# Pool and convolution mixer of a float32 decoder trunk: another order for its second half

## The chip, the cores and the metric

One core of a Trainium2 chip runs the whole program in one launch. The metric is the device time of that launch in microseconds. The engines are TensorE (PE; its weight loads are listed as PEld), VectorE (DVE), ScalarE (ACT), GpSimd (POOL) and SyncE (SP), which here only issues loads. Each engine works through its own list of instructions in order; semaphores tie the lists together.

## The reference, cut to what matters

256 tokens of width 1024 pass two layers in float32: a SwiGLU feed-forward block (FFN), a mixer, another FFN; every part has an RMS norm ahead and adds to the residual `x`. The first layer's mixer is the one that changes:

```python
h = rms_norm(x, mix_norm)
u_pool, u_val, u_gate = split(h @ ab_w_in, (512, 1024))
# pooling: 4 groups of 128 channels, windows 2, 4, 8, 16
mean = trailing_mean(u_pool, window)            # causal
y_pool = einsum('sgc,gcd->sgd', mean - u_pool, pool_w) * pool_scale
# convolution: GLU, depthwise causal conv of 31 taps, LayerNorm over 512 channels, swish
z = conv31(u_val * sigmoid(u_gate), conv_w) + conv_b
mu = mean(z, channels); var = mean((z - mu) ** 2, channels)
y_conv = silu((z - mu) * rsqrt(var + 1e-6) * ln_g + ln_b)
x = x + concat(y_pool, y_conv) @ ab_w_out
```

## The kernel before, in words

**Products in parts.** TensorE multiplies float32 numbers in the faster type fp32r. Each operand is held as a high part (a cast) and a low part (the rest): products high by high, low by high and high by low are summed. So each weight tile takes three steps: the load into `raw` (SyncE), the cast `hi` (ScalarE, L158) and the subtraction `lo` (VectorE, L182). `begin` and `pump` do this. `pump(n)` splits the next n tiles of a fixed list, `stream`, whichever of its two kinds comes next and has a free buffer; `weights(kind)` hands out the next tile and pumps first if it isn't split yet. A tile of kind "gu" (gate/up weights and input projections; 128 x 2048) is split in two halves, one of kind "d" (down and output weights; 128 x 1024) in one piece. There are three raw buffers of each kind, three split ones of "gu" and five of "d". A load is issued when a raw buffer is split (`issue`), a split buffer is free when `done` says that its products are issued and they have run.

**Order.** The schedule is manual: each engine's list has the order in which the code below issues. A `pump` thus puts a cast into ScalarE's list and a subtraction into VectorE's list just where it is called.

**The mixer** (`mixer_ab`, 199 to 289 us). Channels lie on the partitions, tokens along the rows, 128 channels a tile. `wide` makes the first three value/gate pairs; the convolution's taps (L535) run for tile 0, 1, 2, 3 with projections (`narrow_group`, L268) between. `windows` and `pool_diff` (VectorE) make window sums and differences for two pooling groups; `pool_map` (L587, plain float32) maps them, and L591 and L592 scale and split the result into `kh` and `kl`. LayerNorm needs sums over channels, thus over partitions: `mean_mm` (L620) and `variance` (L633) take them on TensorE with a matrix of 1/512, in plain float32. `spread` (L642) brings the reciprocal deviation `r` back to all partitions; `swish` (L656, L658, L652, L653) scales, applies Silu and splits, one token half (`t`) a call. `out_mm(t, k)` adds weight tile k's products (L341) to the accumulators of token half t (two banks each, `a0`, `a1` and `b0`, `b1`): k = 0 to 3 are pooling, 4 to 7 convolution channels, which `tail` does.

**The close and the next FFN.** `tail` finishes token half 0, adds it to `x` (L227, `x_86` and `x_87` are its two column halves), takes sums of squares on ScalarE (L229), `rstd` on GpSimd (L235), `h` on VectorE (L238), and transposes `h` on TensorE (L245) while token half 1's products run; L249 and L252 write the transposed parts into `hT`. Then the next FFN's `wide` starts: first-half-token products of three gate/up tiles (L304), with `finish_b` (the transposes of token half 1) ahead of the third tile, then all of token half 1 (L312) and the low parts (L315).

Of the kernel before, what the change touches and what calls it, by code (L numbers as in the profile page):

```python
# [10 lines left out]
AF = mybir.ActivationFunctionType  # L11
# [28 lines left out]
def tile_trunk(ctx: ExitStack, tc: tile.TileContext, d: dict, out: bass.AP):  # L40
# [20 lines left out]
    def bank(tag):  # L61
        return pspool.tile([P, 512], F32, tag=tag, name=nm(tag), bufs=1)

    def t1():
        return tpool.tile([P, 256], F32, tag="t1", name=nm("t1"), bufs=8)

    def t15():
        return tpool.tile([P, 384], F32, tag="t15", name=nm("t15"), bufs=6)
# [4 lines left out]
    def small(w):  # L73
        return tpool.tile([P, w], F32, tag=f"sm{w}", name=nm("sm"), bufs=8)
# [120 lines left out]
    def done(kind, n=1):  # L195
        spent[kind] += n
# [27 lines left out]
    def norm_half(t, half, accs, coef, ss):  # L224
        x = xs[t][half]
        if accs is not None:
            dve.scalar_tensor_tensor(x, accs[half], coef, x, op0=ALU.mult, op1=ALU.add)  # L227
        junk = tpool.tile([P, 512], F32, tag="bm", name=nm("junk"), bufs=2)
        act.activation(junk, x, AF.Square, scale=1.0 / 32.0, accum_out=ss[:, half:half + 1])  # L229

    def norm_apply(t, ss, g):
        ms = small(1)
        dve.scalar_tensor_tensor(ms, ss[:, 0:1], EPS, ss[:, 1:2], op0=ALU.add, op1=ALU.add)  # L233
        rstd = small(1)
        pool.tensor_tensor(rstd, ms, mhalf[:, 0:1], op=ALU.pow)  # L235
        for half in range(2):
            h = tpool.tile([P, 512], F32, tag="h", name=nm("h"), bufs=4)
            dve.scalar_tensor_tensor(h, xs[t][half], rstd, g[half],  # L238
                                     op0=ALU.mult, op1=ALU.mult)
            yield h  # L240
# [108 lines left out]
    def new_accs():  # L349
        return [[bank(ATAG[t][h]) for h in range(2)] for t in range(2)]  # L350

    def tail(accs, kts, ws, coef, g, units=(1, 1)):

        n = len(kts)

        def mm(t, half, k):
            down_mm(accs[t][half], kts[k], ws[k], t, half, False, k == n - 1)

        ss = small(2)
        for half in range(2):  # L360
            for k in range(n):
                mm(0, half, k)
            pump(units[half])
            norm_half(0, half, accs[0], coef, ss)
        ha = list(norm_apply(0, ss, g))
        for k in range(n):
            mm(1, 0, k)
        for k in range(n):
            mm(1, 1, k)
            if k < 2:  # L370
                transpose_half(0, k, ha, ATAG[0][k])
        done("d", n)
        ss = small(2)
        for half in range(2):
            norm_half(1, half, accs[1], coef, ss)
        hb = list(norm_apply(1, ss, g))

        def finish_b():
            for half in range(2):
                transpose_half(1, half, hb, ATAG[1][half])  # L380
        return finish_b
# [114 lines left out]
    def mixer_ab(finish_b, gname):  # L496
# [13 lines left out]


        where = {}
        ys = [None] * 4
        shifted = {}

# [23 lines left out]
        def taps_out(j):  # L539
            ys[j] = t1()  # L540
            dve.tensor_scalar(ys[j], where[j][:, 0:256], convb[:, j:j + 1], None, op0=ALU.add)

        pw = tpool.tile([P, 512], F32, tag="h", name="pw", bufs=4)
        pool.dma_start(pw, d["pool_w"])
# [66 lines left out]
                done("d")  # L611

        toks = (slice(0, P), slice(P, 2 * P))
        stat = {}

        def mean_mm(js):
            if js[0] == 0:
                stat["mean"] = bank("g2")[:, 0:256]
            for j in js:
                pe.matmul(stat["mean"], ones, ys[j], start=j == 0, stop=j == 3)  # L620

        def squares():
            cs, sqs = [t1() for _ in range(4)], [t15() for _ in range(4)]
            for ts in toks:
                for j in range(4):
                    dve.tensor_tensor(cs[j][:, ts], ys[j][:, ts], stat["mean"][:, ts], op=ALU.subtract)
                    act.activation(sqs[j][:, ts], cs[j][:, ts], AF.Square)
            stat["c"], stat["sq"] = cs, sqs

        def variance(t, tag):  # L630
            var = bank(tag)
            for j in range(4):
                pe.matmul(var[:, 0:1], stat["sq"][j][:, toks[t]], ones[:, 0:1], start=j == 0, stop=j == 3)  # L633
            ve = small(1)
            dve.tensor_scalar(ve, var[:, 0:1], EPS, None, op0=ALU.add)
            r = small(1)
            pool.tensor_tensor(r, ve, mhalf[:, 0:1], op=ALU.pow)
            stat["r", t] = r

        def spread(t, tag):  # L640
            rb = bank(tag)
            pe.matmul(rb[:, 0:P], stat["r", t].to_broadcast([P, P]), ident, start=True, stop=True)  # L642
            stat["rb", t] = rb

        def swish(t):
            ts = toks[t]
            cs, rb = stat["c"], stat["rb", t]
            ss = []

            def lows(j):  # L650
                hi, lo = kts[4 + j]
                (act.copy if j % 2 else dve.tensor_copy)(hi[:, ts], ss[j])  # L652
                dve.tensor_tensor(lo[:, ts], ss[j], f32(hi[:, ts]), op=ALU.subtract)  # L653

            for j in range(4):
                dve.tensor_tensor(cs[j][:, ts], cs[j][:, ts], rb[:, 0:P], op=ALU.mult)  # L656
                s = t1()[:, 0:P]
                act.activation(s, cs[j][:, ts], AF.Silu, scale=lng[:, j:j + 1], bias=lnb[:, j:j + 1])  # L658
                ss.append(s)
                if t == 0:  # L660
                    kts.append(new_split())
                if j >= LAG:
                    lows(j - LAG)
            for j in range(4 - LAG, 4):
                lows(j)
# [27 lines left out]
        taps_pe(1, "b1")  # L693
        taps_out(1)
        load_pack(3)
        p23 = project("a1")
        windows(2, p23)
        taps_pe(2, "b0")
        taps_out(2)
        pump(1)  # L700
        g = load_gain(gname)
        pool_diff(2)
        taps_pe(3, "g1")
        mean_mm((0, 1, 2))
        pump(1)
        taps_out(3)
        preload(AF.Silu)
        p01 = project("g0")
        mean_mm((3,))
        pool_map(2, "g3")  # L710
        squares()
        windows(0, p01)
        variance(0, "g1")
        out_mm(0, 0)
        out_mm(1, 0)
        variance(1, "g2")
        pool_diff(0)
        out_mm(0, 1)
        out_mm(1, 1)
        pool_map(0, "g0")  # L720
        spread(0, "g3")
        spread(1, "g1")
        pump(1)
        swish(0)
        out_mm(0, 2)
        out_mm(1, 2)
        pump(1)
        out_mm(0, 3)
        out_mm(1, 3)
        swish(1)  # L730
        pump(2)
        accs = [accs[0], accs[1]]
        return tail(accs, kts[4:8], [weights("d") for _ in range(4)], 1.0, g, (0, 0))


    def bias_rows(tag):
# [414 lines left out]
```

## Time and profile before

| what | value |
|---|---|
| runs | 990.82, 995.86, 996.42 us (median 995.86) |
| profiled execution, its own time | 993.01 us |
| its span | 991.2 us |
| TensorE, VectorE, ScalarE busy | 98%, 66%, 54% of the span |
| mixer's second half, from the last taps to FFN 1's first matmul | 243.8 to 289.2 us |

[...] Idle time in brackets is the time in which the engine stood still, with the engine and line that ended it.

### The profile page before, as it was taken

The page shows a single profiled execution, that of the slowest core. Times are in us where ns is not written, and L with a number is a line of the kernel's source. Part 1 is how long each engine was busy: PE and PEld are TensorE (multiplying, and loading weights), DVE is VectorE, ACT ScalarE, POOL GpSimd, SP SyncE. Part 2 cuts the span into 40 slices and gives each one's busy share as a digit, 9 for nine tenths or more (in the row PEclk, how much of TensorE's full clock was granted, in tenths as well). Part 3 has the DMA queues.
Part 4 walks back from the last instruction along what each step waited for, and adds up shares of the span by engine and source line. Part 5 has one row for each costly group of instructions (what it writes and reads, how often), then busy time and mean ns, then how long its engine had stood idle before and what let it go on. Part 6 is the DMA issues. An engine that isn't in the chain of part 4 may idle for free.

```text
span 991.2 us, 14724 instructions
## 1 busy us (share of the span) xinstructions
PE 968.1 (98%) x5738; PEld 839.5 (85%) x5738; DVE 657.3 (66%) x1086; ACT 534.0 (54%) x959; POOL 62.9 (6%) x90
## 2 busy tenths in 40 slices
PE   7999999999889999999999999999999999999997
PEld 6888888897769888888988888888889798888885
DVE  6876666678367766666686666667888668666653
ACT  5665555465356655555565555545456646555542
POOL 3000000000000010000000000000435000000000
PEclk9999999999999999999999999999999999999999
DMA  9875555435136656655365555437444616655401
GB/s 332 311 270 191 191 191 191 171 119 173 61 110 240 244 213 237 237 192 206 121 247 209 191 191 191 161 107 264 146 138 157 211 66 242 240 184 195 159 1 43
DMA packets 38021, 182.03 MB, mean 184 GB/s; under 512 B 6416, under 2 KB 6448, under 8 KB 24768
## 3 DMA queue, kind: packets, MB, share of 16 engines
q1 hardware_dynamic: 32400, 169.92, 48.0%
q0 software_dynamic: 5264, 10.92, 3.4%
q8 instruction: 45, 0.74, 0.3%
q10 hardware_dynamic: 288, 0.27, 0.1%
q14 instruction: 24, 0.20, 0.1%
HBM read 179.92 MB, written 4.22 MB: 186 GB/s over the span
## 4 chain that ended last, share of the span: by engine, by line
PE 92%; DVE 3%; issue 2%; ACT 1%; DMA 1%; POOL 0%; SPq 0%; POOLq 0%; DVEq 0%; ACTq 0%
PE g L284 29%; PE g L287 15%; PE a L341 14%; PE b L341 13%; PE g L268 4%; PE g L312 2%; PE g L315 2%; PE g L304 2%; PE a L268 1%; PE b L535 1%; DVE lo L182 1%; PE a L315 1%; PE a L312 1%; PE b L811 1%; DVE keep L957 1%
## 5 line engine op out<-in xcount | busy, mean ns | idle before, releaser
L182 DVE TENSOR_TENSOR lo<-raw,hi 128x1024 fp32r<-128x1024 f32 (+1 forms) x319 | 380.4, 1243 | 56.3 <-ACT hi L158 56.3
L158 ACT CAST hi<-raw 128x1024 fp32r<-128x1024 f32 x320 | 314.8, 1043 | 5.3 <-DMA raw<-in_c_out 3.4
L284 PE MATMUL g<-hT,hi 128*128 128x512 f32 x1248 | 310.7, 391 | 0.8 <-DVE t L327 0.8
L284 PEld LDWEIGHTS g<-hT,hi 128*128 128x128 f32 x1248 | 228.7, 188 | 44.8 <-DVE t L327 1.0
L324 ACT COPY t<-g 128x256 f32<-128x256 f32 x174 | 63.4, 372 | 221.1 <-PE g L287 205.6
L287 PEld LDWEIGHTS g<-hT,lo 128*128 128x128 f32 x1248 | 170.3, 190 | 12.2
L287 PE MATMUL g<-hT,lo 128*128 128x256 f32 x1248 | 174.0, 282 | 0.0
L327 DVE TENSOR_TENSOR t<-g,t 128x256 f32<-128x256 f32 x174 | 71.7, 420 | 137.3 <-ACT t L324 137.3
L341 PE MATMUL a<-hi,kh 128*128 128x512 f32 x208 | 83.4, 401 | 2.8 <-ACT hi L158 2.7
L341 PE MATMUL a<-lo,kh 128*128 128x512 f32 x208 | 82.8, 398 | 1.2 <-DVE lo L182 1.2
L341 PE MATMUL b<-hi,kh 128*128 128x512 f32 x208 | 82.3, 396 | 0.0
L341 PE MATMUL a<-hi,kl 128*128 128x512 f32 x208 | 81.8, 393 | 0.0
L341 PE MATMUL b<-hi,kl 128*128 128x512 f32 x208 | 81.5, 392 | 0.0
L341 PE MATMUL b<-lo,kh 128*128 128x512 f32 x208 | 81.5, 392 | 0.0
L390 ACT CAST kh<-t 128x256 fp32r<-128x256 f32 x88 | 35.7, 406 | 57.6 <-DVE t L388 57.6
L391 DVE TENSOR_TENSOR kl<-t,kh 128x256 fp32r<-128x256 f32 x88 | 37.4, 425 | 41.5 <-ACT kh L390 41.5
L386 ACT ACTIVATE t<-t 128x256 f32<-128x256 f32 x88 | 36.9, 420 | 26.7 <-DVE t L327 26.6
L235 POOL TENSOR_TENSOR sm<-sm,mhalf 128x1 f32<-128x1 f32 x11 | 6.1, 556 | 673.3 <-DVE sm L233 673.3
L341 PEld LDWEIGHTS a<-hi,kh 128*128 128x128 f32 x208 | 39.6, 191 | 10.0 <-ACT hi L158 3.1
L341 PEld LDWEIGHTS a<-hi,kl 128*128 128x128 f32 x208 | 39.5, 190 | 9.0 <-DVE kl L592 0.2
L341 PEld LDWEIGHTS b<-hi,kl 128*128 128x128 f32 x208 | 39.3, 189 | 8.3
L341 PEld LDWEIGHTS b<-hi,kh 128*128 128x128 f32 x208 | 39.4, 189 | 8.2
(208 smaller groups left out, 953.4 us busy)
## 6 DMA issues: line engine op xcount, KB each, us to landing
raw<-in_gu SPq DMA_DIRECT2D x87, 1024.0 KB, 4.9
raw<-in_dn SPq DMA_DIRECT2D x88, 512.0 KB, 5.4
raw<-in_c_qk SPq DMA_DIRECT2D x8, 1024.0 KB, 4.9
raw<-in_ab_in SPq DMA_DIRECT2D x6, 1024.0 KB, 4.8
raw<-in_ab_out SPq DMA_DIRECT2D x8, 512.0 KB, 5.6
raw<-in_c_v SPq DMA_DIRECT2D x8, 512.0 KB, 4.3
raw<-in_c_out SPq DMA_DIRECT2D x8, 512.0 KB, 4.2
eall<-escr POOLq DMA_DIRECT2D x4, 768.0 KB, 17.1
```

The costliest lines, as they stand in the source:

```text
L158: act.copy(hi[:, c], raws[k][:, c])
L182: e.tensor_tensor(lo[:, c], raws[k][:, c], f32(hi[:, c]), op=ALU.subtract)
L268: pe.matmul(dst, wt[:, c, cols], hT[:, c, part, :], start=n == 0, stop=n == len(seq) - 1)
L284: pe.matmul(b, hi[:, c, cols], hT[:, c, 0:2, :], start=c == 0, stop=False, skip_group_check=True)
L287: pe.matmul(b[:, 0:256], lo[:, c, cols], hT[:, c, 0, :], start=False, stop=c == NCH - 1, skip_group_check=True)
L312: pe.matmul(bv[:, :, P:2 * P], w[0][:, c, cs], hT[:, c, 0:2, P:2 * P], start=False, stop=False, skip_group_check=True)
L324: act.copy(t[:m], bv[:, 1, :])
L327: dve.tensor_tensor(dst[:m], bv[:, 0, :], t[:m], op=ALU.add)
L341: pe.matmul(acc, kt[a][:, ts], w[b][:, hs], start=start and n == 0, stop=stop and n == 2)
L386: act.activation(s, gv, AF.Silu)
L390: act.copy(hi, m)
L391: dve.tensor_tensor(lo, m, f32(hi), op=ALU.subtract)
```

## The change

Five things change, all in `mixer_ab` and in the `tail` that it calls. The channel sum of the four convolution tiles is made by adds on VectorE in `taps_out`, and `mean_mm` is one product of that sum; `squares` and `variance` do the same for the squares, on all 256 tokens at once, with the centred values written over `ys`. The last projection's two halves have the first `pool_map` and the mean between them. The second `pool_map` stands between the two token halves of `out_mm(·, 1)`. All four casts in `swish` are ScalarE's, and `swish(1)` stands ahead of `out_mm(·, 3)` in the code. Splits move: one "d" tile ahead of the window sums, none behind `swish(1)`, and `tail` has a new argument, `between`, that pumps one tile behind the first half of the residual sum (other calls of `tail` leave it at 0).

```diff
-    def tail(accs, kts, ws, coef, g, units=(1, 1)):
+    def tail(accs, kts, ws, coef, g, units=(1, 1), between=0):
...
             norm_half(0, half, accs[0], coef, ss)
+            if half == 0:
+                pump(between)
...
         def taps_out(j):
             ys[j] = t1()
             dve.tensor_scalar(ys[j], where[j][:, 0:256], convb[:, j:j + 1], None, op0=ALU.add)
+            if j == 1:
+                stat["sum"] = t1()
+            if j:
+                dve.tensor_tensor(stat["sum"], stat["sum"] if j > 1 else ys[0], ys[j], op=ALU.add)
...
-        def mean_mm(js):
-            if js[0] == 0:
-                stat["mean"] = bank("g2")[:, 0:256]
-            for j in js:
-                pe.matmul(stat["mean"], ones, ys[j], start=j == 0, stop=j == 3)
+        def mean_mm(tag):
+            stat["mean"] = bank(tag)[:, 0:256]
+            pe.matmul(stat["mean"], ones, stat["sum"], start=True, stop=True)
         def squares():
-            cs, sqs = [t1() for _ in range(4)], [t15() for _ in range(4)]
-            for ts in toks:
-                for j in range(4):
-                    dve.tensor_tensor(cs[j][:, ts], ys[j][:, ts], stat["mean"][:, ts], op=ALU.subtract)
-                    act.activation(sqs[j][:, ts], cs[j][:, ts], AF.Square)
-            stat["c"], stat["sq"] = cs, sqs
+            cs, sqs = ys, []
+            for j in range(4):
+                dve.tensor_tensor(cs[j], ys[j], stat["mean"], op=ALU.subtract)
+                sq = t15()[:, 0:256]
+                act.activation(sq, cs[j], AF.Square)
+                sqs.append(sq)
+                if j % 2:
+                    dve.tensor_tensor(sqs[j - 1], sqs[j - 1], sqs[j], op=ALU.add)
+            dve.tensor_tensor(sqs[0], sqs[0], sqs[2], op=ALU.add)
+            stat["c"], stat["sq"] = cs, sqs[0]
-        def variance(t, tag):
+        def variance(tag):
             var = bank(tag)
-            for j in range(4):
-                pe.matmul(var[:, 0:1], stat["sq"][j][:, toks[t]], ones[:, 0:1], start=j == 0, stop=j == 3)
-            ve = small(1)
-            dve.tensor_scalar(ve, var[:, 0:1], EPS, None, op0=ALU.add)
-            r = small(1)
-            pool.tensor_tensor(r, ve, mhalf[:, 0:1], op=ALU.pow)
-            stat["r", t] = r
+            for t in range(2):
+                pe.matmul(var[:, t:t + 1], stat["sq"][:, toks[t]], ones[:, 0:1], start=True, stop=True)
+            ve = small(2)
+            dve.tensor_scalar(ve, var[:, 0:2], EPS, None, op0=ALU.add)
+            r = small(2)
+            pool.tensor_tensor(r, ve, mhalf, op=ALU.pow)
+            stat["r"] = r
...
-                (act.copy if j % 2 else dve.tensor_copy)(hi[:, ts], ss[j])
+                act.copy(hi[:, ts], ss[j])
...
         load_pack(3)
+        pump(1)
         p23 = project("a1")
         windows(2, p23)
         taps_pe(2, "b0")
+        pool_diff(2)
         taps_out(2)
-        pump(1)
         g = load_gain(gname)
-        pool_diff(2)
         taps_pe(3, "g1")
-        mean_mm((0, 1, 2))
-        pump(1)
         taps_out(3)
         preload(AF.Silu)
-        p01 = project("g0")
-        mean_mm((3,))
+        last = weights("gu")
+        b01 = bank("g0")
+        p01 = b01[:, 0:256], b01[:, 256:512]
+        narrow_group(p01[0], last, slice(0, P))
         pool_map(2, "g3")
+        mean_mm("g2")
+        narrow_group(p01[1], last, slice(P, 2 * P))
+        done("gu")
         squares()
-        windows(0, p01)
-        variance(0, "g1")
         out_mm(0, 0)
         out_mm(1, 0)
-        variance(1, "g2")
+        windows(0, p01)
+        variance("g2")
+        out_mm(0, 1)
         pool_diff(0)
-        out_mm(0, 1)
+        pump(1)
+        pool_map(0, "g3")
         out_mm(1, 1)
-        pool_map(0, "g0")
-        spread(0, "g3")
-        spread(1, "g1")
+        spread("g1")
+        swish(0)
         pump(1)
-        swish(0)
         out_mm(0, 2)
         out_mm(1, 2)
         pump(1)
+        swish(1)
         out_mm(0, 3)
         out_mm(1, 3)
-        swish(1)
-        pump(2)
         accs = [accs[0], accs[1]]
-        return tail(accs, kts[4:8], [weights("d") for _ in range(4)], 1.0, g, (0, 0))
+        return tail(accs, kts[4:8], [weights("d") for _ in range(4)], 1.0, g, (0, 0), 1)
```

The lists of three places follow. TensorE behind the last taps, up to the first output products (`g` and `a` are banks, `t` tiles of 256 columns, `kh` and `kl` the split input of a product), before:

```order
L620 MATMUL g_449_2540<-t_419_2274,ones 128x256
L620 MATMUL g_449_2540<-t_426_2381,ones 128x256
L620 MATMUL g_449_2540<-t_439_2487,ones 128x256
L268 MATMUL g_455_2556<-hT,hi_2233 128x256 x16
L268 MATMUL g_455_2556<-hT,lo_2236 128x256 x8
L268 MATMUL g_455_2556<-hT,hi_2233 128x256 x16
L268 MATMUL g_455_2556<-hT,lo_2236 128x256 x8
L620 MATMUL g_449_2540<-t_453_2552,ones 128x256
L587 MATMUL g_456_2606<-t_444_2497,pw 128x256
L587 MATMUL g_456_2606<-t_446_2502,pw 128x256
L633 MATMUL g_474_2653<-ones,t_465_2621 128x1
```

and with the change:

```order
L268 MATMUL g_452_2548<-hT,hi_2233 128x256 x16
L268 MATMUL g_452_2548<-hT,lo_2236 128x256 x8
L594 MATMUL g_453_2573<-t_443_2495,pw 128x256
L594 MATMUL g_453_2573<-t_445_2500,pw 128x256
L624 MATMUL g_458_2584<-t_427_2383,ones 128x256
L268 MATMUL g_452_2548<-hT,hi_2233 128x256 x16
L268 MATMUL g_452_2548<-hT,lo_2236 128x256 x8
L341 MATMUL a_463_2625<-hi_1855,kh_2576 128x512
```

The first map and the one mean product now have half of the projection behind them, and the variance stands behind twelve output products.

VectorE at the mixer's close, from the last low part of `swish(1)` to the norm's `h`, before (`lo_2810` is the last output weight, `lo_2817` a gate/up tile of FFN 1):

```order
L653 TENSOR_TENSOR kl_2751<-t_516_2800,kh_2750 128x128
L182 TENSOR_TENSOR lo_2810<-raw_2493,hi_2808 128x1024
L182 TENSOR_TENSOR lo_2817<-raw_2173,hi_2814 128x1024 x2
L227 SCALAR_TENSOR_TENSOR x_86<-a_477_2662,x_86 128x512
L227 SCALAR_TENSOR_TENSOR x_87<-a_478_2663,x_87 128x512
L233 SCALAR_TENSOR_TENSOR sm_2853<-sm_2822 128x1
L238 SCALAR_TENSOR_TENSOR h_2857<-x_86,sm_2855,gain_2495 128x512
```

and with the change (`lo_2805` is the first gate/up tile of FFN 1):

```order
L664 TENSOR_TENSOR kl_2723<-t_509_2766,kh_2722 128x128
L227 SCALAR_TENSOR_TENSOR x_86<-a_463_2625,x_86 128x512
L182 TENSOR_TENSOR lo_2805<-raw_2106,hi_2802 128x1024 x2
L227 SCALAR_TENSOR_TENSOR x_87<-a_464_2626,x_87 128x512
L233 SCALAR_TENSOR_TENSOR sm_2825<-sm_2786 128x1
L238 SCALAR_TENSOR_TENSOR h_2829<-x_86,sm_2827,gain_2508 128x512
```

The splits ahead of `x_86` are gone, and one stands between `x_86` and `x_87`.

VectorE between the norm of token half 1 and its transposed low part, before:

```order
L238 SCALAR_TENSOR_TENSOR h_2910<-x_88,sm_2908,gain_2495 128x512
L238 SCALAR_TENSOR_TENSOR h_2912<-x_89,sm_2908,gain_2495 128x512
L182 TENSOR_TENSOR lo_2917<-raw_2239,hi_2914 128x1024 x2
L252 TENSOR_TENSOR hT<-b_546_2958,hT 128x4x128
L252 TENSOR_TENSOR hT<-b_547_2965,hT 128x4x128
```

and with the change:

```order
L238 SCALAR_TENSOR_TENSOR h_2882<-x_88,sm_2880,gain_2508 128x512
L238 SCALAR_TENSOR_TENSOR h_2884<-x_89,sm_2880,gain_2508 128x512
L182 TENSOR_TENSOR lo_2889<-raw_2173,hi_2886 128x1024 x2
L182 TENSOR_TENSOR lo_2897<-raw_2239,hi_2894 128x1024 x2
L252 TENSOR_TENSOR hT<-b_539_2938,hT 128x4x128
L252 TENSOR_TENSOR hT<-b_540_2945,hT 128x4x128
```

Two gate/up tiles are split there, where one was; ScalarE's list has their casts in the same place.

## Rows read from the trace of the kernel before

**Rows 1.** The page: span, TensorE's busy time and instructions, gate/up loads (issue to landing, us).

```profile
span 991.2 us, 14724 instructions
...
PE 968.1 (98%) x5738; PEld 839.5 (85%) x5738; DVE 657.3 (66%) x1086; ACT 534.0 (54%) x959; POOL 62.9 (6%) x90
...
raw<-in_gu SPq DMA_DIRECT2D x87, 1024.0 KB, 4.9
```

**Rows 2.** TensorE's timeline behind the last taps: start, duration, instruction, [idle before, releaser].

```profile
243.81 1.56 PE L620 MATMUL g<-t,ones 128*128 128x256 f32 x6
245.03 2.27 PE L268 MATMUL g<-hT,hi 128*128 128x256 f32 x16
...
251.40 1.02 PE L587 MATMUL g<-t,pw 128*128 128x256 f32 x4
255.07 1.05 PE L633 MATMUL g<-ones,t 128*128 128x1 f32 x8 [2.65 <-ACT t L627]
```

**Rows 3.** TensorE's timeline at the mixer's close and FFN 1's start.

```profile
273.53 0.50 PE L341 MATMUL a<-lo,kh 128*128 128x512 f32 x1 [0.47 <-DVE lo L182]
...
276.96 0.50 PE L341 MATMUL a<-hi,kh 128*128 128x512 f32 x1 [2.70 <-ACT hi L158]
278.22 0.80 PE L341 MATMUL a<-lo,kh 128*128 128x512 f32 x1 [0.76 <-DVE lo L182]
...
280.09 0.63 PE L341 MATMUL a<-hi,kl 128*128 128x512 f32 x1
280.52 0.63 PE L341 MATMUL a<-hi,kh 128*128 128x512 f32 x1
...
282.18 0.39 PE L341 MATMUL a<-hi,kh 128*128 128x512 f32 x1
282.40 0.39 PE L341 MATMUL a<-lo,kh 128*128 128x512 f32 x1
...
286.26 0.63 PE L245 MATMUL a<-ident,h 128*128 128x128 f32 x4
...
289.24 4.00 PE L304 MATMUL g<-hT,hi 128*128 128x256 f32 x32
...
296.59 1.34 PE L312 MATMUL g<-hT,hi 128*128 128x256 f32 x8 [0.32 <-DVE hT L252]
```

**Rows 4.** Stretches: length, busy (count) PE PEld DVE ACT POOL, granted clock, DMA, GB/s.

```profile
257.00:259.00 2.00, 2.00 (x7) 1.55 (x6) 0.00 (x0) 0.00 (x0) 0.00 (x0) 0.55 0.03 8
...
279.00:281.00 2.00, 2.00 (x7) 1.54 (x6) 2.00 (x3) 0.00 (x0) 0.00 (x0) 0.50 0.86 246
```

**Rows 5.** VectorE's timeline in the same part of the mixer.

```profile
246.47 0.48 DVE L541 TENSOR_SCALAR t<-g,cpk 128x256 f32<-128x256 f32 x1
...
254.00 0.48 DVE L592 SCALAR_TENSOR_TENSOR kl<-g,cpk,kh 128x256 fp32r<-128x256 f32 x1 [0.54 <-ACT kh L591]
...
268.76 0.67 DVE L656 TENSOR_TENSOR t<-t,g 128x128 f32<-128x128 f32 x3
...
269.86 0.29 DVE L653 TENSOR_TENSOR kl<-t,kh 128x128 fp32r<-128x128 f32 x1
...
276.94 3.50 DVE L182 TENSOR_TENSOR lo<-raw,hi 128x1024 fp32r<-128x1024 f32 x3 [0.19 <-ACT hi L158]
...
283.06 0.69 DVE L227 SCALAR_TENSOR_TENSOR x<-a,x 128x512 f32<-128x512 f32 x1 [2.02 <-PE a L341]
...
295.85 1.28 DVE L252 TENSOR_TENSOR hT<-b,hT 128x512 fp32r<-128x512 f32 x2
```

**Rows 6.** ScalarE's timeline there.

```profile
269.07 1.81 ACT L658 ACTIVATE t<-t,cpk 128x128 f32<-128x128 f32 x4 [1.49 <-DVE t L656]
270.79 0.48 ACT L652 CAST kh<-t 128x128 fp32r<-128x128 f32 x2
...
283.78 0.63 ACT L229 ACTIVATE junk<-x 128x512 f32<-128x512 f32 x1 [1.99 <-DVE x L227]
...
291.30 1.99 ACT L158 CAST hi<-raw 128x1024 fp32r<-128x1024 f32 x2
```

More of the change, by code (lines that the diff above doesn't have):

```diff
@@ L512, in mixer_ab @@
         where = {}
+        stat = {}
         ys = [None] * 4
@@ L613, in mixer_ab @@
         toks = (slice(0, P), slice(P, 2 * P))
-        stat = {}
-        def mean_mm(js):
-            if js[0] == 0:
-                stat["mean"] = bank("g2")[:, 0:256]
-            for j in js:
-                pe.matmul(stat["mean"], ones, ys[j], start=j == 0, stop=j == 3)
-        def squares():
-            cs, sqs = [t1() for _ in range(4)], [t15() for _ in range(4)]
-            for ts in toks:
-                for j in range(4):
-                    dve.tensor_tensor(cs[j][:, ts], ys[j][:, ts], stat["mean"][:, ts], op=ALU.subtract)
-                    act.activation(sqs[j][:, ts], cs[j][:, ts], AF.Square)
-            stat["c"], stat["sq"] = cs, sqs
@@ L630, in variance @@
-        def variance(t, tag):
-            var = bank(tag)
-            for j in range(4):
-                pe.matmul(var[:, 0:1], stat["sq"][j][:, toks[t]], ones[:, 0:1], start=j == 0, stop=j == 3)
-            ve = small(1)
-            dve.tensor_scalar(ve, var[:, 0:1], EPS, None, op0=ALU.add)
-            r = small(1)
-            pool.tensor_tensor(r, ve, mhalf[:, 0:1], op=ALU.pow)
-            stat["r", t] = r
-        def spread(t, tag):
+        def mean_mm(tag):
+            stat["mean"] = bank(tag)[:, 0:256]
+            pe.matmul(stat["mean"], ones, stat["sum"], start=True, stop=True)
@@ L641, in spread @@
+        def variance(tag):
+            var = bank(tag)
+            for t in range(2):
[5 more added lines that the diff above has]
+            stat["r"] = r
+        def spread(tag):
             rb = bank(tag)
-            pe.matmul(rb[:, 0:P], stat["r", t].to_broadcast([P, P]), ident, start=True, stop=True)
@@ L643, in spread @@
-            stat["rb", t] = rb
+            for t in range(2):
+                pe.matmul(rb[:, toks[t]], stat["r"][:, t:t + 1].to_broadcast([P, P]), ident,
+                          start=True, stop=True)
+            stat["rb"] = rb
         def swish(t):
             ts = toks[t]
-            cs, rb = stat["c"], stat["rb", t]
+            cs, rb = stat["c"], stat["rb"]
             ss = []
@@ L651, in lows @@
                 hi, lo = kts[4 + j]
-                (act.copy if j % 2 else dve.tensor_copy)(hi[:, ts], ss[j])
+                act.copy(hi[:, ts], ss[j])
                 dve.tensor_tensor(lo[:, ts], ss[j], f32(hi[:, ts]), op=ALU.subtract)
             for j in range(4):
-                dve.tensor_tensor(cs[j][:, ts], cs[j][:, ts], rb[:, 0:P], op=ALU.mult)
+                dve.tensor_tensor(cs[j][:, ts], cs[j][:, ts], rb[:, ts], op=ALU.mult)
                 s = t1()[:, 0:P]
```

## Prediction

> **What bounds the kernel now.** I read the page first, for who is busy: TensorE works 968.1 of 991.2 us [rows 1], so nearly everywhere a change counts only if it takes work or a wait off TensorE. Next comes TensorE's timeline over the stretch that the diff touches, from the last taps (243.8) to the first matmuls of FFN 1 (L304 at 289.24) [rows 2, 3]. The brackets there are what to look at. TensorE stands still four times: 2.65 us ahead of the variance column (for the squares), then 0.47, 2.70 and 0.76 us ahead of the last output products (for the splits of the last two output weights): 6.6 us. [...] Last come VectorE's and ScalarE's timelines over the same stretch [rows 5, 6], because whoever releases those waits is the bound as soon as TensorE is no longer it.
>
> Behind 296.59 TensorE runs on without gaps, so I take the whole effect to be the shift of that matmul (L312), the first that needs the second token half of FFN 1's input.
>
> **The change on TensorE.** Removed: the four waits, 6.6. The low clock: about 13 products at 0.43 in place of 0.22, so 2.6 to 2.8. Six of the eight passes of the channel mean: the six in front took 243.81 to 245.03, so 1.2. Twelve of the sixteen passes of the variance: eight take 1.05 [rows 2], so 1.5. In all 11.9. The two spreads stay four passes, the two maps stay eight, the output products stay 96. Splitting the projection around map and mean, and the output product around the second map, changes between operand kinds a few times more; the dearest such change seen is about 0.2 (the first sixteen projection matmuls take 2.27 behind the mean, against 4.00 for 32 in L304), so 0 to 0.4, and I take nothing. Were TensorE alone the bound, L304 would start at 277.3.
>
> **What VectorE and ScalarE make of it.** TensorE's own times in the new order, from rows of before: at 243.8 the projection's halves with two mean passes between (251.40 less 245.03, 6.4), the first map 0.9, twelve output products 2.8, four variance passes 0.5, six products 1.5, which is 255.9; then the second map 0.95, six products 1.5 and the spread 0.6 [rows 2, 3]. First half: VectorE gets three adds of about 0.4 and the split of one output weight (1.2) ahead of the last `taps_out`, and loses the two halves of a gate/up split (2.4) there; it ended this at 246.95 [rows 5] and so ends about as early, while TensorE asks for the channel sum only after one projection half and the first map, at about 247.6. Hidden. The first map's scaling takes 2.06 from its end to the last low part (252.42 to 254.48 [rows 2, 5]) and in the new order lies beside the second projection half. The squares follow: four subtractions, four squares, three adds, about 3.7 to 253.4, beside the first twelve output products, which end at about 254.0. So the 2.65 wait goes, with 0.6 to spare. The second map needs the differences at about 256.1 and TensorE comes there at 255.9: 0.1 to 0.2 wait, 0 to 1 by the error of this walk.
>
> From there I follow the path that ends last. Second map's end 257.05, its scaling 2.06, TensorE's spread at 259.1: the first `swish` starts at 259.1. Inside it all four casts are now ScalarE's. From the rows of one `swish` before [rows 5, 6]: the first Silu starts 0.31 after the first product, Silus follow 0.39 apart, the first cast ends at 1.8, its low part (0.29) at 2.1; only then does VectorE reach the fourth product, which stands behind that low part; its Silu ends at 2.85, three casts 0.2 apart at 3.4, the last low part at 3.7. Casts and low parts of the last two output weights come next, 1.0 and 1.2 apart: the second `swish` starts 6.7 after the first, and VectorE reaches the residual sum of token half 0 (`x_86`) at 259.1 + 6.7 + 3.7 = 269.5, though TensorE, with 36 products of 0.228 behind the spread, had that accumulator ready at 267.5. This is the new bound.
>
> Next the split that `between` adds. `x_86` 0.69, its sum of squares 0.72, the two casts 2.0, the second low half 1.2, and small hand-overs: `x_87`, queued behind `lo_2805` on VectorE, starts 4.8 after `x_86`, at 274.3, where TensorE's accumulator has been ready since 270.1. What is queued behind it are the norm, `h`, and TensorE's transposes. In the trace of before, from `x_87` to the transposes is 283.06 to 286.26, 3.2 [rows 3, 5]: they start at 277.4 or 277.5. TensorE is there at 273.5: **a new wait of 3.9**. From the transposes to L304 is 2.98 before, so L304 starts at 280.4: 8.8 earlier than 289.24, not 11.9.
>
> Last the wide stage of FFN 1. One gate/up tile was cast far ahead and one at the mixer's end; now two of three are split between the second norm and its transposes. ScalarE starts these casts 2.06 after L304 (291.30 less 289.24 [rows 3, 6]): the second tile's halves are there at 3.1 and 4.05, the third's at 5.95. TensorE ends the first tile at 1.9, so it waits 1.2 and 0.5. On VectorE two pairs of low halves (2.3 each) stand ahead of the transposed half's low part where one stood; one pair ended at 295.85, 6.6 after L304, so two end at 8.95, and L312, 0.7 to 0.75 behind that, stands 9.65 after L304, against 7.35 before [rows 3, 5]. **2.3 given back.**
>
> Clock: the 3.9 wait is longer than the two that each had a low stretch behind them, so I expect one here. It would lie over the last products and the first tile of L304; the tile's 1.9 lost falls into the 1.7 that TensorE waits anyway, and up to 0.9 of the transposes' side does not. I take 0.3 (0 to 1).
>
> [...]
>
> DMA: the fourth gate/up tile is now asked for only when `lo_2805` frees its buffer, near 273.5, where it was asked for some 27 earlier, and the next two near 287 and 289. They are cast from about 296 on; the profile page's landing time for these loads is 4.9 [rows 1], so they hide. The down-projection loads start earlier than before, since the output weights are split earlier.
>
> Sum: 8.8 - 2.3 - 0.3 = 6.2 earlier. The profiled execution took 993.0 (its span and 1.8 around it), so its like would take 986.8. The three runs have their median 2.9 above it, at 995.86; against that median 6.2 gives **989.7**.
>
> **Rivals.** One: TensorE stays the bound to the end (11.9, so 984.0). It needs `x_86` at the accumulator's end and the added split hidden. For it: VectorE and ScalarE have idle time in these windows. Against: `x_87` is behind `lo_2805` in VectorE's own order, which no idle time elsewhere mends. Two: the first half doesn't come free. If the squares or the second map's differences come 2 later than walked (their prices here are from like forms, no row has them), the variance and the map wait, and everything on the path moves: 4 left, 992. Three, slower than before: the low clock stays. Three waits in 15 us (3.9, 1.7, 1.1) keep TensorE from a closed run of work, and from 277 to 308, where before it ran through the wide stage at full clock, it runs at half: 144 matmuls of 0.12 more each are 17.3, less the 2.8 of waits that this swallows, so 14.5 given back against 6.2 gained: 1004. It decides from the point where the low stretch lasts over some 19 us. Against: both low stretches of before ended after 3 to 4 us, with the engine working as it will here. [...]
>
> **How the numbers follow.** The forecast 0.66 (gain of 4 to 9, for walk errors of a microsecond or two and a low stretch that costs 0 to 1.4); rival one 0.15; rival two 0.14 (gain of 1 to 4); rival three 0.05. The range runs from rival one's 984.0 to rival two's far part, 993.5. About 1% (10 us) is what a measurement of this kernel tells from no change. Over 1% faster: rival one, the forecast's upper edge and the runs' own spread (990.8 to 996.4), 0.24. Over 1% slower: rival three, 0.05. Within: 0.71.
>
> **What would show it.** Right: no wait at the variance, none at the last output products, a quarter of the passes of mean and variance; one wait of 3 to 4 ahead of the first transposes, released by VectorE's `h`; waits for ScalarE's `hi` inside L304 and for VectorE's `hT` at L312, 1 to 1.5 each. Wrong in the path: `x_87` starting within a microsecond of its accumulator, or L304 before 278.5. Wrong in the first half: a wait of more than 1 at variance, second map or spread. Wrong in the cover: a DMA as releaser at a gate/up cast of FFN 1. Wrong in the clock: a granted clock under 0.7 that lasts past L312.

## The result, and the profile after

| | before | changed |
|---|---|---|
| median of 8 runs each | 994.79 us (990.82 to 996.42) | 988.47 us (986.96 to 989.70) |
| profiled execution, its own time | 993.01 | 987.02 |
| its span | 991.2 | 985.3 |

The ratio is 0.994, 95% interval 0.9925 to 0.9955: 6.3 us faster by the medians. The forecast was 989.7 (6.2 faster) in a range of 984.0 to 993.5. The two profiled executions differ by 6.0.

TensorE's timeline of the changed kernel from the last taps to L312, in the columns of [rows 2, 3]:

```profile
243.87 2.18 PE L268 MATMUL g<-hT,hi 128*128 128x256 f32 x16
...
247.72 0.59 PE L624 MATMUL g<-t,ones 128*128 128x256 f32 x2
...
253.77 0.50 PE L642 MATMUL g<-ones,t 128*128 128x1 f32 x4
...
258.23 0.61 PE L652 MATMUL g<-ident,sm 128*128 128x128 f32 x4
...
277.18 0.66 PE L245 MATMUL a<-ident,h 128*128 128x128 f32 x4 [4.03 <-DVE h L238]
...
281.78 2.06 PE L304 MATMUL g<-hT,hi 128*128 128x256 f32 x16
284.48 0.74 PE L304 MATMUL g<-hT,hi 128*128 128x256 f32 x4 [0.64 <-ACT hi L158]
285.43 1.70 PE L304 MATMUL g<-hT,hi 128*128 128x256 f32 x12 [0.21 <-ACT hi L158]
...
291.02 1.33 PE L312 MATMUL g<-hT,hi 128*128 128x256 f32 x8 [1.11 <-DVE hT L252]
```

None of the four waits of before is left (their brackets at 255.07, 273.53, 276.96 and 278.22 in [rows 2, 3]). In their place stand one of 4.03 at the transposes and three small ones in FFN 1's wide stage. The spread starts at 258.23, L304 at 281.78 in place of 289.24 and L312 at 291.02 in place of 296.59.

VectorE's timeline there, to lay beside [rows 5]:

```profile
258.99 0.67 DVE L667 TENSOR_TENSOR t<-t,g 128x128 f32<-128x128 f32 x3
...
269.32 0.69 DVE L227 SCALAR_TENSOR_TENSOR x<-a,x 128x512 f32<-128x512 f32 x1
271.74 2.36 DVE L182 TENSOR_TENSOR lo<-raw,hi 128x1024 fp32r<-128x1024 f32 x2 [1.73 <-ACT hi L158]
274.01 0.68 DVE L227 SCALAR_TENSOR_TENSOR x<-a,x 128x512 f32<-128x512 f32 x1
```

The first `swish` starts at 258.99, `x_86` at 269.32; then VectorE stands still for 1.73 us until the cast of the added split is there, splits for 2.3, and only then takes `x_87`. The chain that ended last (start, length, what) goes the same way: from the first swish to the transposes it runs through VectorE, ScalarE and GpSimd, without TensorE. Its part around the added split:

```profile
269.32 0.70 DVE x L227
...
270.04 0.72 ACT junk L229 x2
270.76 0.95 ACT hi L158
...
271.74 2.36 DVE lo L182 x2
274.10 0.61 DVE x L227
```

The stretches behind the 4.03 wait, in the columns of [rows 4], show the low clock again, 0.50 from 279 to 281:

```profile
277.00:279.00 2.00, 1.82 (x9) 1.49 (x10) 1.30 (x3) 0.59 (x1) 0.00 (x0) 0.74 0.63 258
279.00:281.00 2.00, 2.00 (x8) 1.71 (x7) 0.76 (x2) 0.59 (x1) 0.00 (x0) 0.50 0.00 0
281.00:283.00 2.00, 2.00 (x15) 1.81 (x14) 1.40 (x3) 0.96 (x3) 0.00 (x0) 0.91 0.00 0
```

### The profile page after: what moved, and what is told of

Same layout as the page of the kernel before. It is cut to its first block, busy times and chain, and to the rows that moved or that the text cites. A ratio compares the mean times of both kernels' runs of the same rounds, so it can differ in the third digit from the quotient of the medians.

```text
span 985.3 us, 14682 instructions
## 1 busy us (share of the span) xinstructions
PE 963.4 (98%) x5720; PEld 836.3 (85%) x5720; DVE 658.6 (67%) x1083; ACT 534.3 (54%) x959; POOL 62.3 (6%) x89
## 4 chain that ended last, share of the span: by engine, by line
PE 92%; DVE 4%; ACT 2%; issue 2%; DMA 0%; POOL 0%; SPq 0%; POOLq 0%; DVEq 0%; ACTq 0%
PE g L284 29%; PE g L287 15%; PE a L341 14%; PE b L341 13%; PE g L268 4%; PE g L312 2%; PE g L315 2%; PE g L304 2%; PE a L268 1%; DVE lo L182 1%; PE b L538 1%; PE a L312 1%; PE a L315 1%; PE b L823 1%; DVE keep L969 1%
## 5 line engine op out<-in xcount | busy, mean ns | idle before, releaser
L341 PEld LDWEIGHTS b<-hi,kh 128*128 128x128 f32 x208 | 39.4, 189 | 8.2
L341 PEld LDWEIGHTS b<-lo,kh 128*128 128x128 f32 x208 | 39.4, 189 | 7.8
```

The costliest lines, as they stand in the source:

```text
L341: pe.matmul(acc, kt[a][:, ts], w[b][:, hs], start=start and n == 0, stop=stop and n == 2)
```

## The experiments

Executions differ by up to 2 us in how late the kernel gets going (the last taps end between 243.8 and 245.8), and by as much behind L312 (692.6 to 694.6 us from there to the end of the span), without relation to the edits. So the times of the stretch are given from the end of the last taps, P (the start of TensorE's next product), in one profiled execution each, and go by starts: output products listed at 0.39 start 0.22 apart (282.18 and 282.40 in [rows 3]); the medians and ratios to the kernel before, each with runs of it on the same chip, stand beside them.

The part behind L312 can be read from the traces. At 705 to 725 us, in the second layer's mixer, TensorE waits about 0.9 and then 1.1 us in all twelve traces (in casts_alt the second in two pieces). In six (before, changed, no_between, sums_on_pe, after_old_splits, early_late) a stretch at the low clock follows, and 694.0 to 694.6 us lie between L312 and the end; in the other six none follows, and it is 692.6 to 693.1. The changed kernel and filler in the same 2 us (length, busy (count) of PE, PEld, DVE, ACT and POOL, granted clock, DMA, GB/s):

```profile
715.00:717.00 2.00, 2.00 (x10) 1.94 (x10) 2.00 (x2) 1.29 (x4) 1.15 (x1) 0.50 0.29 100
```

```profile
715.00:717.00 2.00, 2.00 (x18) 2.00 (x18) 2.00 (x1) 1.07 (x4) 1.02 (x1) 1.00 0.24 86
```

The spread of the runs behind the medians goes with the clock as well: over the 30 executions of the kernel before that were measured beside the experiments, spans of 989.5 to 994.7 us go with a mean granted clock of 0.993 to 0.988, and their product stays within 981.6 to 983.6.

| kernel | P | P to L304 | P to L312 | median, us | ratio, 95% interval |
|---|---|---|---|---|---|
| before | 243.81 | 45.43 | 52.78 | 994.8 to 995.5 | |
| changed | 243.87 | 37.91 | 47.15 | 988.47 | 0.994 (0.9925 to 0.9955) |
| early_split | 245.20 | 32.25 | 41.93 | 981.68 | 0.9866 (0.9851 to 0.9882) |
| no_between | 244.66 | 35.37 | 44.18 | 984.68 | 0.9894 (0.9879 to 0.9910) |
| sums_on_pe | 245.78 | 41.62 | 50.91 | 991.21 | 0.9961 (0.9946 to 0.9975) |
| casts_alt | 244.64 | 35.06 | 44.74 | 984.22, one run | |
| before_splits | 245.09 | 46.25 | 55.59 | 995.63 | 1.0008 (0.9995 to 1.0021) |
| after_old_splits | 245.10 | 39.45 | 46.85 | 986.81 | 0.9924 (0.9901 to 0.9947) |
| filler | 244.89 | 36.33 | 46.00 | 985.36 | 0.9901 (0.9882 to 0.9920) |
| early_late | 244.10 | 32.25 | 40.65 | 981.59 | 0.9870 (0.9848 to 0.9892) |
| early_late_alt | 243.94 | 32.11 | 40.52 | 980.38 | 0.9856 (0.9834 to 0.9878) |
| cast_ahead | 244.12 | 32.13 | 39.07 | 977.84 | 0.9830 (0.9811 to 0.9848) |

**early_split: who makes the new wait.** Against the changed kernel:

```diff
         taps_out(3)
+        pump(1)
         preload(AF.Silu)
...
-        return tail(accs, kts[4:8], [weights("d") for _ in range(4)], 1.0, g, (0, 0), 1)
+        return tail(accs, kts[4:8], [weights("d") for _ in range(4)], 1.0, g, (0, 0), 0)
```

> The split of FFN 1's first gate/up tile moves from between x_86 and x_87 to the 2.3 us in which VectorE waits for the first map (246.1 to 248.4 in the changed kernel's trace); nothing else changes. My theory (the changed kernel's 4.03 us wait ahead of the transposes is that split standing in front of x_87): x_87 starts behind its accumulator at about 270.3 in place of 274.0, the wait ahead of the transposes is under 0.5, the low clock behind it is gone, L304 starts at about 276.7 in place of 281.8, L312 9.7 later, and the time is 4 to 5 us under the changed kernel's 988.5. Rival (x_86 is late because of the second swish, and that makes the wait): the wait stays at 2 or more and the gain is under 2 us.

VectorE's `x_86` and `x_87` are now one piece, and TensorE's transposes have no bracket (one row of VectorE's timeline, then TensorE's):

```profile
270.65 1.28 DVE L227 SCALAR_TENSOR_TENSOR x<-a,x 128x512 f32<-128x512 f32 x2
```

```profile
274.43 0.66 PE L245 MATMUL a<-ident,h 128*128 128x128 f32 x4
...
277.45 2.08 PE L304 MATMUL g<-hT,hi 128*128 128x256 f32 x16
280.58 0.74 PE L304 MATMUL g<-hT,hi 128*128 128x256 f32 x4 [1.05 <-ACT hi L158]
...
287.13 1.34 PE L312 MATMUL g<-hT,hi 128*128 128x256 f32 x8 [1.10 <-DVE hT L252]
```

The 4.03 wait is gone whole, L312 comes 5.2 earlier than in the changed kernel. The median is 6.8 lower, where 4 to 5 was expected; the 1.6 over the stretch's 5.2 lie outside it. `x_86` starts as late after P as there (25.45 in both), so the second swish is not what makes the wait: the rival falls. L312 stands 9.68 behind L304, as the prediction's 9.65 had it for a full clock; the granted clock is 1.00 here from 274 to 285.

**no_between: the same split left to FFN 1's start.**

```diff
-        return tail(accs, kts[4:8], [weights("d") for _ in range(4)], 1.0, g, (0, 0), 1)
+        return tail(accs, kts[4:8], [weights("d") for _ in range(4)], 1.0, g, (0, 0), 0)
```

> The split between x_86 and x_87 is left out there and so falls to FFN 1's start, where three gate/up tiles are then split in a row. My theory: the wait ahead of the transposes goes as well (under 0.5), but TensorE now waits some 3 us at L304 for the first cast, and three pairs of low halves stand ahead of the transposed half's low part, so that L312 starts 12 us behind L304 in place of 9.3: L312 at about 289 in place of 291, 1 to 2 us faster than the changed kernel. Rival (the second swish makes the wait, and the split is free cover there): the wait stays, and the third split at FFN 1's start makes it 2 to 3 us slower than the changed kernel.

TensorE's timeline has its one long wait at L304 now, for the first cast:

```profile
280.03 0.74 PE L304 MATMUL g<-hT,hi 128*128 128x256 f32 x4 [2.97 <-ACT hi L158]
280.98 5.11 PE L304 MATMUL g<-hT,hi 128*128 128x256 f32 x28 [0.21 <-ACT hi L158]
288.84 1.34 PE L312 MATMUL g<-hT,hi 128*128 128x256 f32 x8
```

L312 3.0 earlier than in the changed kernel where 1 to 2 was expected: three late splits instead of two still cost less than the one between `x_86` and `x_87`. L312 is 8.8 behind L304, since TensorE's wait now lies ahead of L304, and has no wait of its own.

**sums_on_pe: the channel sums back on TensorE.**

```diff
-            pe.matmul(stat["mean"], ones, stat["sum"], start=True, stop=True)
+            for j in range(4):
+                pe.matmul(stat["mean"], ones, ys[j], start=j == 0, stop=j == 3)
...
-                pe.matmul(var[:, t:t + 1], stat["sq"][:, toks[t]], ones[:, 0:1], start=True, stop=True)
+                for j in range(4):
+                    pe.matmul(var[:, t:t + 1], stat["sq"][j][:, toks[t]], ones[:, 0:1],
+                              start=j == 0, stop=j == 3)
```

(and the six adds in `taps_out` and `squares` left out.)

> The channel sums of values and squares go back to TensorE (four products each that add up in the bank), with every other part of the change kept. My theory: TensorE's work from the last taps to the first swish grows by six mean passes (1.2) and twelve variance passes (1.4), all of it on the path that ends last, so the first swish and all behind it come 2.5 later and the time is 2 to 3 us over the changed kernel's. Rival (VectorE is the bound over this whole stretch, and six adds of 0.4 leave it): no slower, or up to 2 us faster than the changed kernel.

TensorE's timeline:

```profile
249.63 1.89 PE L621 MATMUL g<-t,ones 128*128 128x256 f32 x8
...
256.98 1.84 PE L637 MATMUL g<-ones,t 128*128 128x1 f32 x16
...
281.80 1.11 PE L245 MATMUL a<-ident,h 128*128 128x128 f32 x4 [4.05 <-DVE h L238]
...
287.40 2.18 PE L304 MATMUL g<-hT,hi 128*128 128x256 f32 x16
```

Eight and sixteen passes in place of two and four; a float32 product of 256 columns (two passes) takes 0.39 here, four in 249.63 to 251.17, and one in fp32r 0.13, sixteen of L268 in 251.17 to 253.27. `x_86` comes 28.15 after P (273.93) in place of 25.45: 2.7 later, as expected, and the median is 2.7 over the changed kernel's. In the trace L312 is 3.8 later; the 1.0 more lies between transposes and L304, 5.6 in place of 4.6: the granted clock is at 0.50 from 281 to 287, about twice as long as in the changed kernel.

**casts_alt: the swishes' length.**

```diff
-                act.copy(hi[:, ts], ss[j])
+                (act.copy if j % 2 else dve.tensor_copy)(hi[:, ts], ss[j])
```

> In swish the casts alternate between VectorE and ScalarE again, as in the kernel before; all else as in the changed kernel. My theory (the two swishes lie on the path that ends last, and ScalarE's casts make each 0.4 longer): x_86 starts 0.6 to 0.9 earlier than 269.3, and L304 and L312 by about as much. Rival (they do not lie on it): L304 and L312 stay within 0.2 of 281.8 and 291.

VectorE's and TensorE's row:

```profile
268.83 0.69 DVE L227 SCALAR_TENSOR_TENSOR x<-a,x 128x512 f32<-128x512 f32 x1
```

```profile
276.69 0.66 PE L245 MATMUL a<-ident,h 128*128 128x128 f32 x4 [2.73 <-DVE h L238]
...
279.70 2.07 PE L304 MATMUL g<-hT,hi 128*128 128x256 f32 x16
```

`x_86` 24.19 after P in place of 25.45: 1.3 earlier, more than the 0.6 to 0.9 expected: ScalarE also reaches the next weight casts sooner, 2.1 behind the first swish's first Silu (262.18 less 260.07) in place of 3.0 (262.31 less 259.31). The wait falls from 4.03 to 2.73 and no low stretch follows it (1.00 granted from 274 to 285): from the transposes to L304 3.0 in place of 4.6. So L312 gains 2.4, of which 1.3 is the swishes and the rest the clock. Its time is that of a single run, so the reading rests on the trace.

**before_splits and after_old_splits: one half of the change without the other.** The first is the kernel before with the new places of the splits alone; the second is the changed kernel with the places as before. The edit of the first (with `between` added to `tail` as in the change; the second takes the same lines back):

```diff
         load_pack(3)
+        pump(1)
...
         taps_out(2)
-        pump(1)
...
         mean_mm((0, 1, 2))
-        pump(1)
...
         out_mm(0, 1)
+        pump(1)
         out_mm(1, 1)
...
-        pump(1)
         swish(0)
+        pump(1)
         out_mm(0, 2)
         out_mm(1, 2)
         pump(1)
+        swish(1)
         out_mm(0, 3)
         out_mm(1, 3)
-        swish(1)
-        pump(2)
...
-        return tail(accs, kts[4:8], [weights("d") for _ in range(4)], 1.0, g, (0, 0))
+        return tail(accs, kts[4:8], [weights("d") for _ in range(4)], 1.0, g, (0, 0), 1)
```

> The kernel before with the new places of the weight splits alone (sums on TensorE, order of products and casts as before). Times from the end of the last taps to L312 (before 52.8, changed kernel 47.2). My theory (the new places only move the waits): the 2.70, 0.47 and 0.76 us at the last output products go and with them their low clock, but the split between x_86 and x_87 opens a wait of 3 to 4 at the transposes, and two splits instead of one ahead of the transposed half cost 2.3; the first swish starts at most 1.5 earlier. L312 at 52 to 53, the time within 1 us of before. Rival (the splits' new places are what the change gains): L312 at 49 or less, 4 us or more faster.

> The changed kernel with the places of the weight splits as before (two splits behind the second swish, none between x_86 and x_87). My theory (the gain comes from the first half, up to the first swish, which is 6 us earlier): TensorE waits again for hi and lo of the last output weights, some 4 to 5 us, and has a low stretch behind it, in exchange for the 4.0 us wait and the 2 us at FFN 1's start that go. L312 at 46 to 47.5 us from the last taps' end, within 1.5 us of the changed kernel. Rival (the splits' new places are what the change gains): L312 at 50 or more, the time 4 us or more above the changed kernel.

TensorE's waits in the stretch of before_splits (in total, times, longest):

```profile
PE a L245 <- DVE h L238: 3.7, 1, 3.7
PE g L635 <- ACT t L629: 2.6, 1, 2.6
PE g L312 <- DVE hT L252: 1.1, 1, 1.1
PE g L304 <- ACT hi L158: 1.0, 2, 0.8
```

and of after_old_splits:

```profile
PE a L341 <- ACT hi L158: 3.5, 1, 3.5
PE a L341 <- DVE lo L182: 1.2, 2, 0.8
PE g L624 <- DVE t L548: 0.6, 1, 0.6
PE g L312 <- DVE hT L252: 0.3, 1, 0.3
```

Both ways the new places exchange waits. Alone they make the kernel no faster (ratio 1.0008, its interval about 1). In this trace L312 is even 2.8 later than in before, at 55.6, outside the 52 to 53 expected, and the spread 1.5 later where up to 1.5 earlier was expected: the low stretch behind the variance is about twice as long as the one of before [rows 4]:

```profile
256.00:260.00 4.00, 3.66 (x13) 3.27 (x14) 1.38 (x9) 2.27 (x10) 0.00 (x0) 0.52 0.03 6
260.00:264.00 4.00, 4.00 (x17) 3.28 (x16) 0.43 (x2) 0.60 (x1) 0.00 (x0) 0.62 0.00 0
```

Without them the rest of the change is as fast as with them (0.9924 against 0.994, the intervals overlap), or 1.7 faster by the medians. The rival, that the splits' places are the gain, falls on both sides.

**filler: what the low clock costs.** 16 products into a spare bank in front of the transposes; nobody reads them, so the output is untouched:

```diff
             mm(1, 1, k)
+            if k == 0 and fill:
+                spare = bank("g0")
+                for _ in range(fill):
+                    pe.matmul(spare, kts[0][0][:, 0:P], ws[0][0][:, 0:512], start=True, stop=True)
```

> The changed kernel with 16 products into a spare bank, whose result nobody reads, in front of the transposes, so that TensorE works through most of its 4.03 us wait there. My theory (behind the wait the clock is at its low level and costs time on the path: from the transposes to L304 4.6 us were measured in place of 3.0): the wait is about 0.4, the granted clock stays at 1, transposes to L304 take 3.0 to 3.2, TensorE's waits inside L304 grow from 0.85 to 1.3 or more, and L312 comes 1 to 1.4 earlier than the changed kernel's 47.2 us from the last taps' end. Rival (the low clock is hidden in the waits at L304, as the prediction took it): L312 within 0.4 of 47.2.

```profile
274.01 3.79 PE L375 MATMUL g<-hi,kh 128*128 128x512 f32 x16
278.20 0.66 PE L245 MATMUL a<-ident,h 128*128 128x128 f32 x4 [0.41 <-DVE h L238]
...
281.22 2.08 PE L304 MATMUL g<-hT,hi 128*128 128x256 f32 x16
284.35 0.74 PE L304 MATMUL g<-hT,hi 128*128 128x256 f32 x4 [1.05 <-ACT hi L158]
```

```profile
279.00:281.00 2.00, 2.00 (x13) 1.65 (x12) 1.04 (x2) 1.07 (x2) 0.00 (x0) 1.00 0.12 49
```

TensorE's timeline above, then its clock behind the wait: the useless products fill the wait, the transposes start as late after P as in the changed kernel (33.31 in both), the clock stays at 1.00, transposes to L304 take 3.02, the waits at L304 grow to 1.25 (1.05 and 0.20), and L312 comes 1.15 earlier than in the changed kernel. That is the low clock's price on the path; the median is 3.1 under the changed kernel's, 2 of it within the spread between executions told of above. casts_alt, where no low stretch came either, gains the same beyond its swishes (2.4 less 1.3).

**early_late, early_late_alt, cast_ahead: what remains.** Built on early_split. early_late takes only the casts of FFN 1's second and third tile ahead of the second token half's transposes and puts their low halves behind them on VectorE (`ahead` pumps four tiles there in place of two); early_late_alt adds the alternating casts; cast_ahead also moves the second tile's cast to where ScalarE waits for the first map:

```diff
+    def cast_only(kind):
+        k = state["used"]
+        state["used"] += 1
+        while order[kind].index(k) >= begun[kind]:
+            begin(kind)
+        return parts[k]
...
-            wide([(weights("gu"), list(zip(two, tags[i])), use(i)) for i in range(3)], finish_b)
+            take = [weights] + [cast_only if n == 1 else weights] * 2
+            wide([(take[i]("gu"), list(zip(two, tags[i])), use(i)) for i in range(3)], finish_b,
+                 ahead=4 if n == 1 else 2)
...
         taps_out(3)
         pump(1)
+        begin("gu")
```

> early_split, and in FFN 1's wide stage the low halves of the second and third gate/up tile are put behind the transposed half's low part on VectorE (their casts stay in place). My theory (the wait at L312 is those low halves standing ahead of hT's): the 1.10 wait at L312 goes, the 1.05 and 0.21 at L304 for the casts stay; from the last taps' end to L312 40.8 in place of 41.9, about 1 us faster than early_split. Rival (L312 waits for the casts or the transposes, not for the queue): the wait stays within 0.3 of 1.1.

> early_late with alternating casts in swish, which alone took 1.3 us off the way from spread to x_86 and 2.4 off L312 in the changed kernel. My theory (with the split gone from between x_86 and x_87, TensorE is the bound from the first swish to L304 again, and the swishes no longer lie on the path that ends last): L312 and the time stay within 0.4 us of early_late. Rival (the swishes still lie on it): L312 1 us or more earlier.

> early_late_alt with the cast (not the low half) of FFN 1's second gate/up tile also moved ahead, to where ScalarE waits for the first map. My theory (what is left of TensorE's waits behind the last taps is the 1.06 and 0.21 at L304 for that tile's casts): both go, and L312 comes 1.2 to 1.3 earlier, at 39.2 to 39.4 us from the last taps' end in place of 40.5; the time is 1 us or so under early_late_alt and 15 to 16 under the kernel before. Rival (the third tile's casts or the norm's h take their place): 0.6 or more of the wait stays, at the transposes of token half 1 or the third tile.

early_late's wait at L312 is gone, and L312 is 1.3 earlier than in early_split; its median is no lower (981.59 against 981.68), the microsecond is in the trace alone. early_late_alt has L312 0.13 earlier still (its median is 1.2 lower, which the stretch does not show): with the split gone from between `x_86` and `x_87` the swishes cost nothing, and TensorE is the bound again. In cast_ahead's timeline TensorE has no bracket left from P to behind L312 (`wide` stands seven lines lower here: L311 is the old L304, L319 the old L312):

```profile
276.25 3.99 PE L311 MATMUL g<-hT,hi 128*128 128x256 f32 x32
...
283.19 1.12 PE L319 MATMUL g<-hT,hi 128*128 128x256 f32 x8
```

L312 stands at 39.07, where 39.2 to 39.4 was expected. At 977.84 us, 17 to 18 under the kernel before and 10.6 under the changed kernel, it is the version that beats both.

## Why the prediction was right, point by point

**The path.** It was walked from rows of before, and held nearly row for row: first swish 259.1 forecast, 258.99 measured; `x_86` 269.5 and 269.32; `x_87` 274.3 and 274.01; transposes 277.4 and 277.18; the new wait 3.9 and 4.03. That this wait is the split's own is shown by early_split, which moved nothing else and removed it whole; the filler and casts_alt changed what lay around it and kept the split, and `x_87` stayed 4.7 behind `x_86` in both.

**The first half.** Hidden adds and squares, as forecast: no wait at the variance, the sum's product at 247.72 without a bracket. The sums were put at 1.2 + 1.5 and are worth 2.7 (sums_on_pe). Rival two falls with it.

**The splits' places.** Here the prediction's books were right and its emphasis was not: it credited the change with 6.6 us of waits removed and debited 3.9 and 2.3 elsewhere. The pair before_splits and after_old_splits shows that 3.9 of those 6.6 (2.70, 0.47, 0.76) were exchanged for the new ones and brought nothing. The change's gain is the way from P to the spread: 14.36 now (243.87 to 258.23) in place of 21.13, 6.8 less. Of these, 2.7 are the sums' (sums_on_pe); the other 4.1 fit the 2.65 wait and one low stretch at 1.4 (half of the 2.6 to 2.8 that the prediction took for two), but no run takes them apart. TensorE's row for the spread in the kernel before:

```profile
264.94 0.61 PE L642 MATMUL g<-ident,sm 128*128 128x128 f32 x4
```

**FFN 1's start.** L312 9.65 behind L304 was forecast, 2.3 given back. It is 9.68 and 9.67 where the granted clock around L304 is 1.00 (early_split, filler) and 9.24 in the changed kernel: there the slow products ahead of L304 (0.50 granted from 279 to 281) hold it back against ScalarE's list, whose casts start 1.62 behind it (283.40) in place of 2.05 (filler, 283.27 less 281.22). The two waits for casts were put at 1.2 and 0.5 and are 1.05 and 0.21 at a full clock. early_late shows that the queue on VectorE, not the casts, held up L312.

**The clock: the term that was mis-sized.** In the kernel before, 0.55 and 0.50 were granted in 2 us behind each of the two long waits [rows 4], and products started 0.43 apart there (280.09 and 280.52) and 0.22 apart at 282.18 and 282.40 [rows 3]; the 2.6 to 2.8 for the two stretches are the prediction's estimate from these starts. For a new stretch it took 0.3 (0 to 1): it put the stretch over the last products and L304's first tile and let most of it fall into TensorE's waits there. It cost 1.15 (filler). The stretch, with 0.50 granted in 279 to 281 behind the 4.03 wait, lay ahead of L304, over the products between the transposes, 4.6 in place of 3.0, where each us counts; the first tile's sixteen products took 2.06, as at the full clock of early_split (2.08). Only 0.4 came back, in shorter waits for the casts (0.85 in place of 1.25). One stretch at half the price of the two, 1.4, which is the upper end in the prediction's chances, was nearer.

**Rival one** (TensorE stays the bound, 11.9) is what the kernel does once the split is moved: L304 is then 13.2 to 13.3 earlier after P (45.43 to 32.25 and 32.13). The 11.9 was short by 1.3; the starts behind each wait and the variance passes at the low clock were not counted, but no run tells their shares. **Rival three** (the low clock stays) had no sign: the granted clock was at 0.91 in the stretch 281 to 283 and at 1.00 behind it, up to 310. That waits so close together hold the clock low was the author's supposition; no run shows it. DMA was no releaser of any wait in the stretch, as the cover by loads had it.

**The sum.** 8.8 - 2.3 - 0.3 = 6.2 was forecast; from P, L304 came 7.5 and L312 5.6 earlier, and the medians 6.3 apart. In the forecast's own terms the stretch gives 9.1 - 2.3 - 1.15 = 5.6: the transposes came 0.3 earlier than forecast, FFN 1's start cost at a full clock what was forecast, and the clock cost 0.85 more. That the medians meet the forecast within 0.1 is luck: the rest of their 6.3 lies outside the stretch, where executions differ by up to 2 us with their low stretches. These are as large as some of the edits, which is why the shares above go by the trace's stretch and not by medians. The prediction took 1% as the least that can be told from no change; the interval here is 0.15% to either side.

## What to carry to other kernels

A split, copy or cast that is queued between two halves of a norm can cost its whole chain (here cast and subtraction, 4 us of waiting for 2.3 us of VectorE work), even where both engines have idle time (VectorE 34%, ScalarE 46% of the span before); put it where its engine already waits for something else. When waits vanish at one place, look along each engine's list for where the same work now stands before concluding that they are saved: run each half of the change alone. A TensorE wait like those here is to be charged with a possible low stretch behind it (0 to 2.6 us ahead of L304 in these traces), and in full wherever TensorE's next work is on the path.

## What the runs showed of the hardware

In these traces the wait's length alone does not tell whether a low stretch follows it. Waits of 2.65 and 2.70 (before), 2.97 (no_between) and 4.03 (changed) each had one behind them (0.55, 0.50, 0.52 and 0.50 granted in 2 us of it), and so had, in six of twelve traces, the pair of 0.9 and 1.1 in the second layer; the 2.73 of casts_alt had none, with the granted clock at 1.00 throughout:

```profile
274.00:277.00 3.00, 0.31 (x3) 0.31 (x4) 1.48 (x4) 0.72 (x2) 0.55 (x1) 1.00 0.72 248
277.00:279.00 2.00, 2.00 (x14) 1.71 (x12) 0.99 (x2) 1.08 (x2) 0.00 (x0) 1.00 0.36 152
```

Its length differs as well: behind the same 4.0 wait, transposes to L304 took 4.6 in the changed kernel and 5.6 in sums_on_pe, against 3.0 without a low stretch. By these traces such a term is a range from 0 to 2.6 us ahead of L304, and nothing in the rows read here told beforehand where in it a wait would fall.
